# The RWKV scan of a hybrid encoder: inverse blocks reordered, DMAs merged, one engine's stores moved, the hand-written order of the pieces changed

## The chip, the cores and the metric

The kernel runs on one core of a Trainium2 chip. The metric is the device time of one execution in microseconds (us), the median of the runs shown; lower is better. The core has TensorE (PE, with PEld for its weight loads), VectorE (DVE), ScalarE (ACT), GpSimd (POOL) and SyncE (SP), each with its own instruction queue that runs in program order. All DMAs of the kernel before but one are issued from SP's queue.

## What is computed

Two layers, each a token mixer and a convolutional feed-forward block on a residual of 512 tokens by 1024 channels in float32. Layer 0 mixes by windowed attention, layer 1 by the bidirectional RWKV-7 scan, 16 heads of 64, and the change is in that scan alone. Its core:

```python
def wkv7_scan(r, w, k, v, a, bb, reverse):
    ...
    def step(state, inp):
        r_t, w_t, k_t, v_t, a_t, b_t = inp
        sa = jnp.einsum('bhvk,bhk->bhv', state, a_t)
        state = state * w_t[:, :, None, :] + sa[..., None] * b_t[:, :, None, :] + v_t[..., None] * k_t[:, :, None, :]
        y = jnp.einsum('bhvk,bhk->bhv', state, r_t)
        return state, y
    s0 = jnp.zeros((b, nh, n, n), F32)
    _, y = lax.scan(step, s0, seq, reverse=reverse)
    return jnp.moveaxis(y, 0, 1)
...
    y_f, bonus_f = direction(0)
    y_b, bonus_b = direction(1)
    y = y_f + y_b
```

After the scan come a norm per head, a bonus term, a gate and the output projection `w_o`.

## The kernel before, in words

Activations are held transposed, [channel, token]; channels come in KT = 8 tiles of 128, so one "tile of heads" is two heads (e = 0, 1) in two directions (d = 0, 1). Tokens are cut into NC = 8 chunks of 64. The time recurrence is rewritten by chunk: inside a chunk it is a triangular system, so for each chunk, head and direction a 64x64 unit triangular matrix has to be inverted. It is split into two halves h of 32: 2 halves x 2 directions x 8 chunks x 2 heads = 64 blocks of 32x32 for one tile of heads.

`rwkv_proj` (L432) makes the operands and stores them to DRAM (`ars`, `bks`, `vs`); near its end it already runs the first pieces of the scan for two tiles of heads (`stages`, L1172). `rwkv_scan.run` (L1209) then runs the scan, software-pipelined: i goes from -1 to 7, and in each i the eight strings of `K.between` (L1313) are played out, one per chunk step j. I call the strings slots 0 to 7, and the time from one w0 to the next a period. The pieces of a string:

- c: `step` (L1106), chunk step j of tile i: state matmuls (L1115, L1119), the products of the next chunk (`added`, L1104), and on VectorE the decay of the state (L1117), on which the matmuls of the next step wait.
- l0 to l3: `low` (L928), the triangular matrices of tile i+2: matmuls L937, masked eviction on VectorE L939. b: `blocks` (L942) stores the 32x32 blocks to DRAM (`ls`, L946, 4 DMAs) and loads them, one block to a partition, into both halves of the tile X (L950, 2 DMAs, which wait for the stores).
- G3, V5, V6, G4, g4, g5: so many steps of `solve` (L986) on GpSimd (G, g) or VectorE (V). G and V work for tile i+2, g and v for tile i+1. 31 steps (kx = 31 down to 1), each a multiply (L1000) and an add (L1002) over 16 to 136 elements; the 32nd call ends the inverse: four copies X<-Y on ScalarE (L905 by `copy`) and four stores `zs` from SP (L1012).
- I: `inverses` (L1022) loads the inverse blocks back, 2 DMAs for T32 (tile t, L1028) and 8 for TT (tt, L1032); L0, L1: `level` (L1034), the off-diagonal quarter, ends in four copies tt (L905).
- u: the loads vv of the values (L958, 3 DMAs); t0, t1: transposes L966 with copies bw on ScalarE; a0, a1: `sides` (L970, matmuls L976, L978, copies xa, xv on ScalarE); x0, x1 (L1070, copies x, then vv, on ScalarE) and m0, m1 (L1079, VectorE L1082, L1083): `batch` (L1060) for chunks 0-3 and 4-7; w0, w1: `locals_` (L1096).
- n0 to n4: the head norm of tile i-1: square on ScalarE (L1139), sum on VectorE (L1142), power on GpSimd (L1144), scaling on VectorE (L1146), PE transposes (L1151), VectorE L1154, L1155, store os (L1159). e: loads gt, bo. p: `prep` (L913) loads the operands of tile i+3.

At the end of `run` every instruction is chained to the one before it on its engine, so each queue, SP's too, keeps the order in which the pieces stand. `bank()` hands out four PSUM banks in turn; a piece waits until the evictions of the one four banks earlier are done.

Of the kernel before, what the change touches and what calls it, by code (L numbers as in the profile page):

```python
# [8 lines left out]
F32 = mybir.dt.float32  # L9
# [806 lines left out]
def rwkv_scan(K, A, sc, mid):  # L816
# [9 lines left out]
    MID = ("gc", "ks", "mask", "id2", "t", "gt", "bo")  # L826
    PLACE = {"early": ("bw0", "ar0", "ar1", "bk0", "bk1", "X0", "Y0", "tg", "tv"),
             "ring": ("bw1", "ar2", "ar3", "bk2", "bk3", "xa0", "vv", "mt0", "qt0", "mt1", "qt1", "st", "rv", "tt0", "Q", "x10", "x11", "t32"),
             }
# [4 lines left out]
    def qr(e, h):  # L834
        return slice(HD * e + 32 * h, HD * e + 32 * h + 32)
# [34 lines left out]

    GROUPS = [(hf, d) for hf in range(2) for d in range(2)]
    BOTH = [(d, e) for d in range(2) for e in range(2)]
# [16 lines left out]
    def inputs(n, bks=True):  # L889

        for _ in range(n):
            for _ in range(2):
                R.ARs.append(mk([P, 2, NC, HD], f"ar{len(R.ARs)}"))
                if bks:
                    R.BKs.append(mk([P, NC, 2, HD], f"bk{len(R.BKs)}"))
            R.BWs.append(mk([P, 2, NC, 2, 3 * HD], f"bw{len(R.BWs)}").rearrange("p d c e s -> p c d e s"))
# [16 lines left out]
    def prep(ct):  # L913

        c = Ctx()
        c.AR, c.BK = [], []
        for d in range(2):
            c.AR.append(R.ARs[(2 * ct + d) % len(R.ARs)])
            nc.sync.dma_start(out=c.AR[d], in_=sc["ar"][ct, d])
            c.BK.append(R.BKs[(2 * ct + d) % len(R.BKs)])  # L920
            nc.sync.dma_start(out=c.BK[d], in_=sc["bk"][ct, d])
        return c
# [18 lines left out]

    def blocks(ct, c):  # L942

        for d in range(2):
            for h in range(2):
                nc.sync.dma_start(out=sc["l"][ct, d, h].rearrange("c e i j -> i c e j"),  # L946
                                  in_=c.BW[qr(d, h), :, d, :, 32 * h:32 * h + 32])
        c.X = block()
        for h in range(2):
            nc.sync.dma_start(out=c.X[er(h)], in_=sc["l"][ct].rearrange("d h c e i j -> (d h c e) i j"))  # L950

# [34 lines left out]
    def solve(ct, c):  # L986
# [18 lines left out]
        for h in range(2):  # L1005
            yh = Y[HD * h:HD * h + HD]
            copy("z0", h, Z[0:HD].rearrange("p i (j h) -> p i j h", h=2)[:, :, :, h], yh)
            copy("z1", h, Z[HD:P].rearrange("p (j h) i -> p j h i", h=2)[:, :, h], yh.rearrange("p i j -> p j i"))
        zd = sc["z"][ct]
        for i, d in ((0, 0), (0, 1), (1, 0), (1, 1)):  # L1010
            p0 = d + HD * (i == 0)
            nc.sync.dma_start(out=zd[i, :, d], in_=Z[p0:p0 + HD - d:2])  # L1012

# [158 lines left out]
    def stages(names):  # L1172

        for x in names:
            ct = R.done[x]
            R.done[x] += 1
            K.ct = ct
            if x == "p":
                R.cs.append(prep(ct))
            elif x == "l":  # L1180
                for g in range(4):
                    low(ct, R.cs[ct], g)
                blocks(ct, R.cs[ct])
            else:
                go(ct, R.cs[ct], 32, "G")
# [5 lines left out]
    def part(i, q):  # L1191
# [69 lines left out]
def body(ctx, tc, A, out, stage=9):  # L1261
# [109 lines left out]
    def ffn(layer, xT, st, nxt, nst, store):  # L1371
# [152 lines left out]
```

## Time and profile before

| | us |
|---|---|
| median of 3 runs | 1620.83 |
| lowest, highest | 1620.26, 1624.76 |
| the profiled execution | 1621.33 |
| its span | 1619.5 |
| the scan's periods (first to last w0 in the trace) | 926.9 to 1165.3 |
| PE busy over the span | 92% |
| DVE, ACT, POOL busy over the span | 63%, 43%, 28% |
| granted TensorE clock, mean | 0.938 |

The span is the part of the execution with instructions in it; 1.8 us lie around it. Outside the scan PE is busy nearly all the time; the slices in which it is not, and in which the granted clock falls to about half and then hovers around eight tenths, are those from about 850 to 1200 us.

### The profile page before, as it was taken

The numbers are of one execution on the slowest core, as the hardware profiler recorded it, in microseconds if no ns is written. First come the engines' busy times: TensorE is split into PE (matmuls) and PEld (weight loads), VectorE is DVE, ScalarE is ACT, GpSimd is POOL, SyncE is SP. The second block draws the span as 40 slices with busy tenths as digits, with TensorE's granted clock in tenths as the row PEclk, the third lists the DMA queues.
The fourth block names the chain that finished last, engine by engine and source line by source line (L and its number), as shares of the span: only waits on it lengthen the run. The fifth ranks groups of instructions, "written<-read, shape, count | busy, mean of one in ns | idle before, by whom it ended". The sixth has DMA issues, their size and how long they took to land.

```text
span 1619.5 us, 28606 instructions
## 1 busy us (share of the span) xinstructions
PE 1494.3 (92%) x11612; PEld 1203.0 (74%) x11612; DVE 1024.9 (63%) x1652; ACT 689.1 (43%) x1147; POOL 449.7 (28%) x546
## 2 busy tenths in 40 slices
PE   8999999999999998989987588888689999999999
PEld 7767688888888886667765477777567788888887
DVE  6876447777763348968878556676256677777222
ACT  5576434444442223655545243434324444444111
POOL 2630002322210015425696423334100323222000
PEclk9999999999999999999975688888789999999999
DMA  5200032232333322346627545555532222333331
GB/s 192 73 27 1 25 94 92 91 103 93 100 91 119 112 81 71 127 156 234 206 88 225 156 117 150 151 136 145 160 106 82 88 92 94 93 103 101 100 121 56
DMA packets 110131, 180.15 MB, mean 111 GB/s; under 512 B 50096, under 2 KB 63024, under 8 KB 110000
## 3 DMA queue, kind: packets, MB, share of 16 engines
q1 hardware_dynamic: 109856, 178.33, 36.0%
q8 instruction: 91, 1.49, 0.4%
q14 instruction: 40, 0.33, 0.1%
q10 hardware_dynamic: 144, 0.00, 0.0%
HBM read 142.91 MB, written 35.39 MB: 110 GB/s over the span
## 4 chain that ended last, share of the span: by engine, by line
PE 69%; DVE 11%; DMA 6%; POOL 5%; issue 4%; ACT 4%; SPq 1%; POOLq 0%; ACTq 0%; DVEq 0%
PE mm L106 16%; PE mm L104 16%; PE mm L105 16%; PE mm L387 2%; PE sc L104 2%; PE sc L105 2%; PE sc L106 2%; PE tp L382 2%; DVE wlo L71 2%; POOL Y L1002 1%; POOL tg L1000 1%; PE sc L367 1%; DMA X<-ls 1%; DVE sf L530 1%; PE bank L1096 1%
## 5 line engine op out<-in xcount | busy, mean ns | idle before, releaser
L68 ACT CAST whi<-wraw 128x1024 fp32r<-128x1024 f32 (+2 forms) x196 | 200.4, 1023 | 270.2 <-PE mm L105 178.4
L104 PE MATMUL mm<-hl,whi 128*128 128x512 f32 x720 | 281.7, 391 | 1.5 <-DVE xT L1354 0.9
L106 PE MATMUL mm<-hl,wlo 128*128 128x512 f32 x720 | 281.5, 391 | 0.6 <-POOL wlo L71 0.4
L105 PE MATMUL mm<-hl,whi 128*128 128x512 f32 x720 | 281.4, 391 | 0.4 <-DVE hl L92 0.4
L71 DVE TENSOR_TENSOR wlo<-wraw,whi 128x1024 fp32r<-128x1024 f32 (+2 forms) x139 | 170.7, 1228 | 174.6 <-ACT whi L68 173.9
L71 POOL TENSOR_TENSOR wlo<-wraw,whi 128x1024 fp32r<-128x1024 f32 x57 | 137.1, 2406 | 414.8 <-ACT whi L68 414.8
L185 DVE SCALAR_TENSOR_TENSOR conv<-upad,par,conv 128x512 f32<-128x512 f32 x88 | 125.6, 1429 | 64.0 <-ACT conv L182 64.0
L106 PEld LDWEIGHTS mm<-hl,wlo 128*128 128x128 f32 x720 | 135.6, 188 | 31.9 <-POOL wlo L71 2.3
L104 PEld LDWEIGHTS mm<-hl,whi 128*128 128x128 f32 x720 | 135.7, 189 | 29.6 <-ACT hl L91 1.3
L105 PEld LDWEIGHTS mm<-hl,whi 128*128 128x128 f32 x720 | 135.7, 189 | 29.5 <-DVE hl L92 1.1
L106 PE MATMUL mm<-gh,wlo 128*128 128x512 f32 x352 | 139.0, 395 | 0.0
L104 PE MATMUL mm<-gh,whi 128*128 128x512 f32 x352 | 139.0, 395 | 0.0
L105 PE MATMUL mm<-gl,whi 128*128 128x512 f32 x352 | 139.0, 395 | 0.0
L1000 POOL TENSOR_TENSOR tg<-X,Y 128x56 f32<-128x56 f32 (+9 forms) x136 | 51.5, 379 | 142.4 <-DMA X<-ls 67.9
L97 ACT CAST gh<-gact 128x512 fp32r<-128x512 f32 x44 | 27.3, 621 | 141.4 <-DVE gact L194 141.4
L182 ACT ACTIVATE conv<-upad,par 128x512 f32<-128x512 f32 x88 | 71.6, 815 | 21.5 <-DVE upad L180 21.3
L106 PEld LDWEIGHTS mm<-gh,wlo 128*128 128x128 f32 x352 | 66.1, 188 | 16.1
L105 PEld LDWEIGHTS mm<-gl,whi 128*128 128x128 f32 x352 | 66.1, 188 | 16.0
L104 PEld LDWEIGHTS mm<-gh,whi 128*128 128x128 f32 x352 | 66.1, 188 | 16.0
L187 DVE SCALAR_TENSOR_TENSOR conv<-upad,par,conv 128x512 f32<-128x512 f32 x88 | 70.0, 798 | 3.0
L192 ACT ACTIVATE silu<-conv 128x512 f32<-128x512 f32 x44 | 27.8, 632 | 91.3 <-DVE conv L187 91.3
L106 PE MATMUL mm<-sx,wlo 128*128 128x512 f32 (+1 forms) x144 | 59.9, 416 | 5.2 <-DVE wlo L71 5.0
(334 smaller groups left out, 3078.5 us busy)
## 6 DMA issues: line engine op xcount, KB each, us to landing
wraw<-in_w_up_dram SPq DMA_DIRECT2D x88, 512.0 KB, 3.6
wraw<-in_w_down_dram SPq DMA_DIRECT2D x32, 512.0 KB, 3.5
ars<-tab SPq DMA_DIRECT2D x16, 512.0 KB, 2.7
bks<-tab SPq DMA_DIRECT2D x16, 512.0 KB, 3.0
ar<-ars SPq DMA_DIRECT2D x16, 512.0 KB, 5.1
bk<-bks SPq DMA_DIRECT2D x16, 512.0 KB, 6.4
wraw<-in_w_down_dram SPq DMA_DIRECT2D x16, 384.0 KB, 3.2
wraw<-in_w_qkv_dram SPq DMA_DIRECT2D x11, 512.0 KB, 4.5
```

The lines of the kernel that those rows point to most:

```text
L68: nc.scalar.copy(out=hi, in_=raw)
L71: lo_engine.tensor_tensor(out=lo, in0=raw, in1=hi.bitcast(F32), op=ALU.subtract)
L104: nc.tensor.matmul(ps, lhsT=lhs[0], rhs=rhs[0], start=first, stop=False)
L105: nc.tensor.matmul(ps, lhsT=lhs[0], rhs=rhs[1], start=False, stop=False)
L106: nc.tensor.matmul(ps, lhsT=lhs[1], rhs=rhs[0], start=False, stop=last)
L182: nc.scalar.activation(out=c, in_=u[:, 1:S + 1], func=AF.Identity, scale=K.par[:, cw + 2 * FT + ch:cw + 2 * FT + ch + 1], bias=K.par[:, cb ...
L185: nc.vector.scalar_tensor_tensor(out=c, in0=u[:, 0:S], scalar=K.par[:, cw + ch:cw + ch + 1], in1=c, op0=ALU.mult, op1=ALU.add)
L187: nc.vector.scalar_tensor_tensor(out=c, in0=u[:, 2:S + 2], scalar=K.par[:, cw + 4 * FT + ch:cw + 4 * FT + ch + 1], in1=c, op0=ALU.mult, op ...
L192: nc.scalar.activation(out=sg, in_=acts[0], func=AF.Silu)
L382: nc.tensor.transpose(out=tp[:, j * P:(j + 1) * P], in_=p[:, e, j * P:(j + 1) * P], identity=K.ident)
L387: nc.tensor.matmul(po[e * HD:(e + 1) * HD, n], lhsT=vn[:, n - 1 + j, kv * HD:(kv + 1) * HD], rhs=pT[:, e, j * P:(j + 1) * P], start=n == 0 ...
L1000: en.tensor_tensor(out=tm, in0=X[:, 0:kx, kx:kx + 1].broadcast_to([P, kx, n]), in1=Y[:, kx:kx + 1, m:16].broadcast_to([P, kx, n]), op=ALU. ...
```

## The change

Three things are changed in the data and one in the order. The 64 blocks are ordered (half, direction, chunk, head) where they were (direction, half, chunk, head); the stores `ls` of one direction are issued as soon as its two `low` pieces are done (b0, b1, with GROUPS reordered to go by direction); the inverse goes back to DRAM in 3 DMAs issued by ScalarE, holding of the transposed part only the blocks that are read (384 KB where it was 512 KB); TT is loaded in 4 DMAs of twice the size. The operands AR and BK of both directions come in one DMA each. TT has two buffers, its copies alternate between ScalarE and VectorE. Both x pieces and a1 stand late in the period before, and the steps of the inverse are dealt out anew.

```diff
-    GROUPS = [(hf, d) for hf in range(2) for d in range(2)]
+    GROUPS = [(hf, d) for d in range(2) for hf in range(2)]
...
-            for _ in range(2):
-                R.ARs.append(mk([P, 2, NC, HD], f"ar{len(R.ARs)}"))
-                if bks:
-                    R.BKs.append(mk([P, NC, 2, HD], f"bk{len(R.BKs)}"))
+            R.ARs.append(mk([P, 2, 2, NC, HD], f"ar{len(R.ARs)}"))
+            if bks:
+                R.BKs.append(mk([P, 2, NC, 2, HD], f"bk{len(R.BKs)}"))
...
-        for d in range(2):
-            c.AR.append(R.ARs[(2 * ct + d) % len(R.ARs)])
-            nc.sync.dma_start(out=c.AR[d], in_=sc["ar"][ct, d])
-            c.BK.append(R.BKs[(2 * ct + d) % len(R.BKs)])
-            nc.sync.dma_start(out=c.BK[d], in_=sc["bk"][ct, d])
+        nc.sync.dma_start(out=bk, in_=sc["bk"][ct].rearrange("d p c z s -> p d c z s"))
+        nc.sync.dma_start(out=ar, in_=sc["ar"][ct].rearrange("d p z c s -> p d z c s"))
...
-    def blocks(ct, c):
-
-        for d in range(2):
-            for h in range(2):
-                nc.sync.dma_start(out=sc["l"][ct, d, h].rearrange("c e i j -> i c e j"),
-                                  in_=c.BW[qr(d, h), :, d, :, 32 * h:32 * h + 32])
-        c.X = block()
+    def blocks(ct, c, d):
+
         for h in range(2):
-            nc.sync.dma_start(out=c.X[er(h)], in_=sc["l"][ct].rearrange("d h c e i j -> (d h c e) i j"))
+            nc.sync.dma_start(out=sc["l"][ct, h, d].rearrange("c e i j -> i c e j"),
+                              in_=c.BW[qr(d, h), :, d, :, 32 * h:32 * h + 32])
+        if d:
+            c.X = block()
+            for b in range(2):
+                nc.sync.dma_start(out=c.X[er(b)], in_=sc["l"][ct].rearrange("h d c e i j -> (h d c e) i j"))
...
+            copy("z1", h, Z[HD:P].rearrange("p (j h) i -> p j h i", h=2)[:, :, h], yh.rearrange("p i j -> p j i"))
+        for h in range(2):
+            yh = Y[HD * h:HD * h + HD]
             copy("z0", h, Z[0:HD].rearrange("p i (j h) -> p i j h", h=2)[:, :, :, h], yh)
-            copy("z1", h, Z[HD:P].rearrange("p (j h) i -> p j h i", h=2)[:, :, h], yh.rearrange("p i j -> p j i"))
         zd = sc["z"][ct]
-        for i, d in ((0, 0), (0, 1), (1, 0), (1, 1)):
-            p0 = d + HD * (i == 0)
-            nc.sync.dma_start(out=zd[i, :, d], in_=Z[p0:p0 + HD - d:2])
+        for d in range(2):
+            nc.scalar.dma_start(out=zd[0, 48 * d:48 * d + 16], in_=Z[HD + 48 * d:HD + 48 * d + 16])
+        nc.scalar.dma_start(out=zd[1], in_=Z[0:HD])
...
-        for e in range(2):
-            for h in range(2):
-                for d in range(2):
-                    nc.sync.dma_start(out=c.TT[qr(e, h), :, d, 32 * h:32 * h + 32], in_=zs[1, d, h, :, e].rearrange("c i j -> i c j"))
+        for h in range(2):
+            for e in range(2):
+                nc.sync.dma_start(out=tt[qr(e, h), :, :, 32 * h:32 * h + 32].rearrange("p d c s -> p (d c) s"),
+                                  in_=sc["z"][ct, 1, 32 * h + e:32 * h + 32:2].rearrange("b i j -> i b j"))
...
-        R.TTs = [mk([P, NC, 2, HD], "tt0")]
-        eng("zero").memset(R.TTs[0], 0.0)
+        R.TTs = [mk([P, 2, NC, HD], f"tt{i}") for i in range(2)]
+        for t in R.TTs:
+            eng("zero").memset(t, 0.0)
...
         if x in "xm":
-            k, fn, args = i + (args[0] == 0), batch, [args[0], int(x == "m")]
+            k, fn, args = i + (q != "m1"), batch, [args[0], int(x == "m")]
...
-    K.between = ("w0 c l0 l1 u g4", "c l2 l3 b e g5", "c x1 I", "c m1 w1 n0 G3", "c t0 t1 n1 V5", "c a0 a1 n2 V5 p", "c L0 n3 V6", "c L1 x0 n4 m0 G4")
+    K.eng["tt"] = "CV"
+    K.between = ("w0 c l0 l1 b0 u g5", "c l2 l3 g6 b1 I", "c m1 w1 n0 e", "c t0 t1 n1 G4", "c a0 p V5 n2", "c L0 n3 V4", "c L1 a1 n4 G4", "c x0 x1 m0 G4")
```

## Rows read from the trace of the kernel before

**Rows 1.** Windows of the periods: us, busy by engine (x count), PEclk, DMA share, GB/s.

```profile
1133.10:1165.30 32.20, 25.15 (x675) 21.48 (x672) 9.13 (x23) 14.04 (x30) 6.41 (x17) 0.82 0.43 109
sum 238.40, PE 200.28 PEld 173.26 DVE 139.45 ACT 98.65 POOL 76.39; mean PE 28.61 PEld 24.75 DVE 19.92 ACT 14.09 POOL 10.91
```

**Rows 2.** PE's waits, 910 to 1175 us: total us, times, longest.

```profile
PE bank L1104 <- ACT vv L905: 12.8, 14, 4.7
PE bank L1119 <- DVE st L1117: 5.3, 4, 2.1
PE pre L1044 <- DMA tt<-zs: 2.6, 2, 1.5
```

**Rows 3.** Timeline, one period from 1031.7: start, us; the blocks to DRAM and back.

```profile
1038.92 2.04 SPq L946 DMA_DIRECT2D ls<-bw  x4
1042.72 1.11 SPq L950 DMA_DIRECT2D X<-ls  x2
1048.37 0.25 POOL L1000 TENSOR_TENSOR tg<-X,Y 128x31 f32<-128x31 f32 x1 [12.52 <-DMA X<-ls]
```

**Rows 4.** Timeline, the same period: the inverse, VectorE, GpSimd and ScalarE.

```profile
1050.35 1.65 POOL L1144 TENSOR_TENSOR rv<-rv,mhalf 128x8 f32<-128x8 f32 x1
1053.29 0.68 DVE L1146 TENSOR_TENSOR t<-t,rv 128x512 f32<-128x512 f32 x1
1061.20 0.41 POOL L1000 TENSOR_TENSOR tg<-X,Y 128x120 f32<-128x120 f32 x1 [9.20 <-DVE Y L1002]
1061.75 0.90 DVE L1155 TENSOR_TENSOR t<-t,gt 128x512 f32<-128x512 f32 x1
1062.19 0.74 POOL L1000 TENSOR_TENSOR tg<-X,Y 128x121 f32<-128x121 f32 x1
1071.44 3.47 ACT L905 COPY X<-Y 64x512 f32<-64x512 f32 x4 [7.52 <-POOL Y L1002]
```

**Rows 5.** Timeline, 1039 to 1063: PE's pieces, and ScalarE's copies behind them.

```profile
1039.37 1.10 PE L1070 MATMUL mm<-xa,tt 64*64 64x128 f32 x32
1050.87 1.07 ACT L905 COPY xa<-mm 128x512 f32<-128x512 f32 x2 [1.01 <-PE mm L976]
1052.58 1.07 ACT L905 COPY xa<-pre 128x512 f32<-128x512 f32 x2 [0.63 <-PE pre L978]
1054.52 1.15 PE L1151 MATMUL bank<-ident,t 64*64 64x64 f32 x32
1057.67 0.75 PE L1044 MATMUL mm<-tt,Q 32*32 32x32 f32 x64
1058.94 3.13 PE L1070 MATMUL pre<-xa,tt 64*64 64x128 f32 x32 [0.51 <-ACT tt L905]
1062.38 1.54 ACT L905 COPY vv<-pre 64x256 f32<-64x256 f32 x4
```

**Rows 6.** Groups by form, 900 to 1140: a solve operation on VectorE and GpSimd, mean ns.

```profile
L1000 DVE TENSOR_TENSOR tv<-X,Y 128x126 f32<-128x126 f32 x21 | 6.0, 288 | 0.5
L1002 POOL TENSOR_TENSOR Y<-Y,tg 128x121 f32<-128x121 f32 x7 | 2.9, 418 | 0.6
```

**Rows 7.** Windows, columns as in Rows 1: the vv loads in the DMA queues.

```profile
1032.00:1034.00 2.00, 2.00 (x54) 1.93 (x52) 1.61 (x5) 0.00 (x0) 1.56 (x6) 0.84 1.00 205
1034.00:1036.00 2.00, 2.00 (x48) 1.84 (x44) 1.09 (x2) 0.91 (x2) 1.52 (x7) 1.00 0.10 16
```

**Rows 8.** DMA issues: KB each, median us to landing.

```profile
vv<-vs SPq DMA_DIRECT2D x8, 256.0 KB, 7.0
```

**Rows 9.** Windows, columns as in Rows 1: PE's longest wait and the clock behind it.

```profile
1138.80:1142.00 3.20, 0.00 (x0) 0.00 (x0) 0.25 (x1) 2.89 (x4) 0.22 (x1) 0.98 0.00 0
1143.50:1148.60 5.10, 4.81 (x72) 4.07 (x72) 1.56 (x5) 1.03 (x3) 0.00 (x0) 0.50 0.68 137
```

**Rows 10.** Timeline ahead of the scan, 877 to 901 us: SP's queue and VectorE.

```profile
877.09 3.81 SPq L1012 DMA_DIRECT2D zs<-X  x4
900.79 1.72 DVE L766 TENSOR_TENSOR tab<-tr,ts 128x512 f32<-128x512 f32 x1 [5.57 <-DMA ars<-tab]
```

More of the change, by code (lines that the diff above doesn't have):

```diff
@@ L826, in rwkv_scan @@
     MID = ("gc", "ks", "mask", "id2", "t", "gt", "bo")
-    PLACE = {"early": ("bw0", "ar0", "ar1", "bk0", "bk1", "X0", "Y0", "tg", "tv"),
-             "ring": ("bw1", "ar2", "ar3", "bk2", "bk3", "xa0", "vv", "mt0", "qt0", "mt1", "qt1", "st", "rv", "tt0", "Q", "x10", "x11", "t32"),
+    PLACE = {"early": ("bw0", "ar0", "bk0", "X0", "Y0", "tg", "tv"),
+             "ring": ("bw1", "ar1", "bk1", "xa0", "vv", "mt0", "qt0", "mt1", "qt1", "st", "rv", "tt0", "tt1", "Q", "x10", "x11", "t32"),
              }
@@ L915, in prep @@
         c = Ctx()
-        c.AR, c.BK = [], []
-        for d in range(2):
-            c.AR.append(R.ARs[(2 * ct + d) % len(R.ARs)])
-            nc.sync.dma_start(out=c.AR[d], in_=sc["ar"][ct, d])
-            c.BK.append(R.BKs[(2 * ct + d) % len(R.BKs)])
-            nc.sync.dma_start(out=c.BK[d], in_=sc["bk"][ct, d])
+        ar, bk = R.ARs[ct % len(R.ARs)], R.BKs[ct % len(R.BKs)]
+        c.AR, c.BK = [ar[:, d] for d in range(2)], [bk[:, d] for d in range(2)]
+        nc.sync.dma_start(out=bk, in_=sc["bk"][ct].rearrange("d p c z s -> p d c z s"))
+        nc.sync.dma_start(out=ar, in_=sc["ar"][ct].rearrange("d p z c s -> p d z c s"))
         return c
@@ L1022, in inverses @@
     def inverses(ct, c):
-        zd = sc["z"][ct]
         c.T32 = mk([P, NC, 2, 32], "t32", 1)
-        c.TT = R.TTs[ct % K.ntt]
-        zs = zd.rearrange("x (d h c) e i j -> x d h c e i j", d=2, h=2)
+        tt = R.TTs[ct % len(R.TTs)]
+        c.TT = tt.rearrange("p d c s -> p c d s")
         for d in range(2):
-            nc.sync.dma_start(out=c.T32[qr(d, d)], in_=zs[0, d, d].rearrange("c e i j -> i c e j"))
-        for e in range(2):
-            for h in range(2):
-                for d in range(2):
-                    nc.sync.dma_start(out=c.TT[qr(e, h), :, d, 32 * h:32 * h + 32], in_=zs[1, d, h, :, e].rearrange("c i j -> i c j"))
+            nc.sync.dma_start(out=c.T32[qr(d, d)].rearrange("p c e s -> p (c e) s"), in_=sc["z"][ct, 0, 48 * d:48 * d + 16].rearrange("b i j -> i b j"))
+        for h in range(2):
+            for e in range(2):
+                nc.sync.dma_start(out=tt[qr(e, h), :, :, 32 * h:32 * h + 32].rearrange("p d c s -> p (d c) s"),
+                                  in_=sc["z"][ct, 1, 32 * h + e:32 * h + 32:2].rearrange("b i j -> i b j"))
     def level(ct, c, k):
@@ L1182, in stages @@
                     low(ct, R.cs[ct], g)
-                blocks(ct, R.cs[ct])
+                for d in range(2):
+                    blocks(ct, R.cs[ct], d)
             else:
@@ L1378, in body @@
           "bo": dram.tile([KT, P, S], F32, name="bos"), "o": dram.tile([KT, P, S], F32, name="os"),
-          "l": dram.tile([KT, 2, 2, NC, 2, 32, 32], F32, name="ls"), "z": dram.tile([KT, 2, 32, 2, 32, 32], F32, name="zs")}
+          "l": dram.tile([KT, 2, 2, NC, 2, 32, 32], F32, name="ls"), "z": dram.tile([KT, 2, HD, 32, 32], F32, name="zs")}
     st = {}
```

## The prediction

> **What bounds the kernel now.** I read the page's slices first: PE is busy nearly throughout except from about 850 to 1200 us, the scan, which is all that the change touches. Then the windows from one w0 to the next. Seven periods take 238.40 us, 34.1 each, PE is busy 28.6 of them, and the last, in which no new inverse is begun, takes 32.2; the six with one average 34.4 [rows 1]. A busy PE is not yet a bound here: x0 takes 3.13 us where the same 32 matmuls as x1 take 1.10 [rows 5], the granted clock being 1.2 GHz in the one and 2.4 in the other, beside a first matmul that waits for copies. At full clock and without waits PE would need some 24 us of a period (28.6 by the granted 0.84 or so).
>
> So a period is set by chains that go once round through the in-order queues. PE's waits name their ends: for ScalarE's vv copies, for the state on VectorE, for the TT loads [rows 2]. The timeline of one period shows the links. From w0 at 1031.7 the blocks' stores start at 7.2 us, the X loads are issued at 11.0 and GpSimd begins to solve at 16.7, having idled for it [rows 3]. Three steps later (2.0) VectorE takes over, does sixteen steps, and GpSimd resumes at 29.5 and ends at 39.7, when ScalarE begins the four copies, 3.5 us [rows 4]. Those copies stand ahead of x1's copies on ScalarE, which is why PE waits for vv, 12.8 us in all [rows 2].
>
> **The change, part by part.**
>
> Merged and moved DMAs. SP issues per tile fall from 30 to 20 (TT 8 to 4, operands 4 to 2, the inverse's 4 to ScalarE); the bytes of the inverse fall by a quarter. In the steady scan this takes TT's landing off PE's path (2.6 us in all, [rows 2]), some 0.4 a period. Ahead of the scan it is worth more: the four z stores hold SP for 3.81 us, and VectorE later sits 5.57 us behind an operand store that queued after such traffic [rows 10]. I take 4.5 us off there; bounds 0 (another wait ends last) and 6. On ScalarE three issues cost, by SP's own, 0.51 each (ls, [rows 3]) to 0.95 (z, [rows 10]); I take 1.5 us, since the queue it goes to is empty.
>
> A rule that speaks against this part: the Trainium skill, DMA: Bandwidth & Descriptors, section Issuing engines are not separate DMA queues, says that DMAs started on different engines end on the same 16 DMA engines, and that a second issuer saves only the sequencer's time. By that rule the move is worth the issue time alone; the sum above takes no more.
>
> x1 out of the wait. x1 goes from slot 2 to slot 7 of the period before, ahead of the inverse's copies. PE's 12.8 us of waiting for vv over seven tiles, 1.8 a period, go. What is late next is the subject of the rest.
>
> The step counts. Per tile VectorE does 9 steps where it did 16, GpSimd 22 where it did 15. An operation of this size takes 288 ns on VectorE and 418 on GpSimd [rows 6]; a step is (61.2 - 50.4 - 1.3 for three other operations) / 16 = 0.59 us on the one and, for the largest that GpSimd does now, 62.19 - 61.20 = 0.99 on the other [rows 4]. Seven steps at 0.4 us: 2.8 us more in the chain of the inverse.
>
> Another rule against it: the Trainium skill, SBUF — State Buffer, section Who interferes with whom, says that a VectorE instruction with two SBUF inputs and a GpSimd instruction that reads SBUF exclude each other. The trace agrees: the one GpSimd operation that meets L1155 takes 0.74 us where its neighbour takes 0.41 [rows 4]. More solve steps on GpSimd meet L1155 and L1146; that would add 0.3 a period, which I leave in the range.
>
> The new order, slots 0 to 5. Here I expect the loss. PE now does, ahead of n3: w0, six chunk steps, l0 to l3, m1, w1, t0, t1, a0, L0. That is x1 and a1 less than before, and the vv wait less: against n3 at 22.8 us after w0 now (1054.52, [rows 5]), less 1.1 (x1), 1.7 (a1), 1.8 (vv) and 0.8 (the wait for the state, 5.3 over seven, [rows 2]), PE stands before n3 at 17.4. But n3 needs n2, and n2 stands on VectorE behind V5, V5 behind G4 on GpSimd, G4 behind X. The X loads need the last stores of b1, which need the last eviction of l3: nothing of that chain is shortened. So n3 can begin at X + 2.7 (four steps at 2.0/3) + 2.9 (five at 0.59) + 0.7 (L1146): X + 6.3, or 23.0 us with X at 16.7. **PE idles 5.6 us in one piece.**
>
> X itself may come later. In SP's order u now stands behind b0, whose stores wait for the evictions of l0 and l1 (some 5.5 us after w0, by estimate: the first stores of now, which need l2 too, start at 7.2, [rows 3]), where it stood behind nothing. Its loads are 512 KB in short packets and land 7.0 us after issue [rows 8]; now they fill the DMA engines for about 2 us (share 1.00) and are over by 1034 [rows 7], well before the stores of the blocks at 1038.9. Issued at about 6.6 to 8.5 us they run just ahead of b1's stores and X on the same queue. Bounds: 0, if they are through, and 3; I take 1.5, so X at 18.2.
>
> Slots 5 to 7. Behind n3 stand n3 1.15, a chunk step and L1 0.8 each, a1 1.7 (the second pair of xa copies starts 1.7 after the first), the xa copies 1.07, x0 1.10, then, since x0, x1 and m0 take turns on four banks, six copies x and vv at 1.54/4 each, 2.3, which hide x1, and m0 1.1 like x1 [rows 5]: 10.0 us. The period at full clock is 18.2 + 6.3 + 10.0 = 34.5; with X at 16.7, 33.0.
>
> The clock. After PE's longest wait the granted clock is at 0.50 for 5.1 us of work behind it, having been at 0.98 while PE stood still [rows 9]. A wait of 5.6 to 7 us in every period does the same, and the work in those 5.1 us takes half of that longer: 2.5 us. What shorter waits cost at the period's end they cost today too (x0 at 3.13). **Period: 34.5 + 2.5 = 37.0**, against 34.4.
>
> The sum. Six periods by 2.6 is 15.6. Off: 4.5 ahead of the scan; at the end of the scan the last tile's inverse comes back by fewer DMAs, 2 (0 to 4). On: x1 in the first round, 1.5. 15.6 - 4.5 - 2 + 1.5 = +10.6. The profiled execution took 1621.33 us, 0.5 above the median; its span with 1.8 around it would become 1632, the median 1631.
>
> **The rivals.** First, faster. If u's loads don't delay X and the clock recovers early (PE's stretch behind n3 not slowed), the period is set by another chain round GpSimd and ScalarE: eighteen GpSimd steps, twelve of which take 10.2 and the six larger ones 1.0 each, 16.2; the copies 3.5 [rows 4]; three issues 1.5; the square and sum of the norm, by L1146's size 0.7 each, 1.4; the power 1.65; G4 2.7; V5 2.9; L1146 0.7; V4 2.4 [rows 4]: 33.0, with state operations and hops 33.7. That is a floor whatever PE does. Six times -0.7, and -5 around it: -9, 1612. It decides from a PE stretch behind n3 of at most 10.5 us. For it: every edit in isolation removes a wait. Against it: the wait of 5.6 us and what the clock does behind one.
>
> Second, no change: the clock costs 2.5 but X stays at 16.7: 35.5, six by 1.1 = 6.6, less 5: 1622. For it: the vv loads are only 2 us of full queue, and today's run behind 2 MB of operand loads.
>
> Third, worse: the clock stays low to the end of the period, as it is at x0 and m0 now: the 6 us of PE work behind n3 cost up to 4.5 rather than 2.5: 39.0, six by 4.6 = 27.6, less 5: 1643.
>
> That the change does nothing (merged loads off the path, queues still in the same chain) falls under the second: it would give 1620 to 1622.
>
> **How the numbers follow.** Forecast, 1631: 0.38. Faster, 1612: 0.30. No change, 1622: 0.22. Worse, 1643: 0.10. Faster by over 0.3% (4.9 us, about what can be told from no change) has the first rival, 0.30; within 0.3% the second, 0.22; slower 0.48. The range goes from 1606, the faster case with 6 us won ahead of the scan and 4 at its end, to 1641, the forecast with half of the worse case: 1606 to 1641. For slower alone 1626 to 1643.
>
> **What would show it.** Right: PE idle 4 us or more before L1151 in every period, released by L1146; the 0.50 clock behind it; the vv loads in the queue between the two pairs of ls stores; GpSimd's first solve step 17.5 or more after w0. No PE wait for vv is left. Wrong: periods of 34 or less, or L1151 reached by PE only after 22 us, so that nothing waits there. The part ahead of the scan is right if the first w0 comes before 926.9 by 2 us or more.

## The result

The changed kernel takes 1642.36 us (median of four runs, 1641.39 to 1642.77) where the kernel before takes 1620.55 (four runs on the same chip). The ratio is 1.0129, 95% interval 1.011 to 1.0148. The forecast was 1631, 1606 to 1641: the direction is right, the loss is twice what was forecast.

Where it went is read from the windows between one w0 and the next. First the kernel before, in three stretches (first period, the five that carry a whole tile, the last); then the changed kernel. Columns are those of [rows 1]: start:end, us, busy by engine, PEclk, DMA share, GB/s.

```profile
926.90:959.00 32.10, 27.03 (x707) 23.39 (x704) 18.02 (x55) 13.61 (x29) 8.28 (x28) 0.87 0.49 129
959.00:1133.10 174.10, 148.10 (x3683) 128.39 (x3680) 112.31 (x315) 71.00 (x150) 61.69 (x171) 0.84 0.53 138
```

```profile
928.40:963.90 35.50, 24.87 (x706) 22.22 (x704) 15.08 (x43) 12.78 (x28) 13.02 (x40) 0.86 0.48 121
963.90:1156.00 192.10, 134.11 (x3682) 119.16 (x3681) 97.32 (x255) 67.20 (x141) 91.39 (x241) 0.83 0.53 124
1156.00:1185.00 29.00, 21.87 (x676) 19.05 (x674) 9.99 (x25) 13.36 (x29) 8.03 (x21) 0.88 0.34 82
```

The first w0 comes 1.5 us later, the first period is 3.4 longer, the five full periods 18.0 (38.4 each where they took 34.8), the last 3.2 shorter than that of [rows 1], and what follows 1.2 longer: 20.9, the difference of the two spans (1640.4 and 1619.5). In the five, PE is busy 14 us less at about the same granted clock and GpSimd 30 more: the time is waiting.

The waits of PE from 928 to 1156 (total, times, longest), in answer to [rows 2]:

```profile
PE bank L1149 <- DVE t L1144: 22.4, 5, 4.6
PE pre L1039 <- DMA t<-zs: 12.4, 4, 4.8
PE mm L1039 <- DMA t<-zs: 12.3, 5, 4.8
PE bank L1113 <- DVE st L1115: 5.3, 6, 4.1
```

The row for vv that led [rows 2] is gone, as is that for TT; what is left of waiting for vv are twelve waits of at most 0.5 before m0 and m1 (L1077), 5.0 us in all. In their place PE stands still twice in each full period: 4.4 to 4.6 us before n3 (L1149), which was forecast, and 2.4 to 4.8 before L0 (L1039), for T32, which was not. The two have one cause, and it is on SyncE's queue. One period, w0 at 1040.3, answering [rows 3] (start, us; SyncE, then ScalarE, then GpSimd):

```profile
1045.60 0.86 SPq L942 DMA_DIRECT2D ls<-bw  x2
1046.56 1.94 SPq L955 DMA_DIRECT2D vv<-vs  x3
1053.08 0.90 SPq L942 DMA_DIRECT2D ls<-bw  x2
1055.96 1.57 SPq L947 DMA_DIRECT2D X<-ls  x2
1057.58 1.11 SPq L1026 DMA_DIRECT2D t<-zs  x2
...
1048.48 2.87 ACT L904 COPY X<-Y 64x512 f32<-64x512 f32 x3 [7.18 <-POOL Y L999]
1050.67 1.26 ACTq L1010 DMA_DIRECT2D zs<-X  x2
1052.03 0.45 ACTq L1011 DMA_DIRECT2D zs<-X  x1
...
1061.29 0.25 POOL L997 TENSOR_TENSOR tg<-X,Y 128x31 f32<-128x31 f32 x1 [4.65 <-DMA X<-ls]
```

The last block of l3 is evicted 8.0 us after w0, and the queue is free at 1048.5. Yet b1's two stores are issued only 12.8 us after w0, X 15.7 (11.0 before, [rows 3]), and the first solve step comes at 21.0 instead of 16.7. The waits of SyncE's queue say for what:

```profile
SPq L942 <- DMA zs<-X: 23.6, 8, 4.5
SPq L947 <- DMA ls<-bw: 8.1, 8, 1.8
```

The ls stores wait 23.6 us for DMAs of zs, which they neither read nor write. The built program tells why. Each DMA, whichever engine issues it, adds to one of eight counters in turn, and waits until the DMA eight numbers before it, the last on its counter, has landed. The numbers are given when the program is built, by the order in which the builder reckons that the DMAs will be issued. It reckons the three z stores ahead of the period's first ls store; on the chip ScalarE issues them 5 us behind it. One period of the listing (number, issuer, counter, what it waits for):

```
332 ACT zs<-X  counter 3   the copies of Z, 324 tt<-zs
333 ACT zs<-X  counter 4   325 tt<-zs
334 ACT zs<-X  counter 5   the copies of Z, 326 tt<-zs
335 SP  ls<-bw counter 6   l0, l1 and 327 gt<-gs
336 SP  ls<-bw counter 7   328 bo<-bos
...
340 SP  ls<-bw counter 3   l2, l3 and 332 zs<-X
341 SP  ls<-bw counter 4   333 zs<-X
342 SP  X<-ls  counter 5   335, 336, 340, 341 and 334 zs<-X
```

So the blocks of tile i+2 wait for the inverse of tile i+1 to be stored. With the z stores on SyncE, as before, the numbers could not run ahead of the queue.

### The profile page after: what moved, and what is told of

Its sections match the earlier page's. It is cut to its first block, busy times and chain, and to the rows that moved or that the text cites. A ratio compares the mean times of both kernels' runs of the same rounds, so it can differ in the third digit from the quotient of the medians.

```text
span 1640.4 us, 28397 instructions
## 1 busy us (share of the span) xinstructions
PE 1476.3 (90%) x11612; PEld 1191.6 (73%) x11612; DVE 1006.3 (61%) x1570; ACT 683.5 (42%) x1131; POOL 491.8 (30%) x645
## 3 DMA queue, kind: packets, MB, share of 16 engines
q8 instruction: 91, 1.49, 0.4%
## 5 line engine op out<-in xcount | busy, mean ns | idle before, releaser
L997 POOL TENSOR_TENSOR tg<-X,Y 128x56 f32<-128x56 f32 (+20 forms) x185 | 70.4, 381 | 93.4 <-DVE Y L999 42.8
L999 POOL TENSOR_TENSOR Y<-Y,tg 128x56 f32<-128x56 f32 (+20 forms) x185 | 77.6, 420 | 13.3
```

The source lines that it names most:

```text
L997: en.tensor_tensor(out=tm, in0=X[:, 0:kx, kx:kx + 1].broadcast_to([P, kx, n]), in1=Y[:, kx:kx + 1, m:16].broadcast_to([P, kx, n]), op=ALU. ...
L999: en.tensor_tensor(out=Y[:, 0:kx, m:16], in0=Y[:, 0:kx, m:16], in1=tm, op=ALU.add)
```

## The experiments

Two theories for the five periods. **N**, the numbered wait: solve, Z, z store, ls store, X and the next solve have become a closed loop (a chain that comes back to its own first step one tile later), and its length is the period. **O**, the order, the prediction's reason: X is late for the vv loads ahead of it, and PE waits for n2 behind V5. For the stretch ahead of the scan the theories come below. In this table the times are read from each trace; "X" is the first solve step after w0 and "n3" its start after w0, both the mean of the five full periods. The ratio is that of all runs; the times are those of one execution, which can lie some us off its kernel's median (e7's 3.4 below, e3's 3.0 below, e8's 3.6 above); if all of that lay in the scan, it would be up to 0.6 us a period. The first w0 of the changed kernel and of e3 are 1.0 apart, though the engines do the same up to there.

| kernel | ratio to before, 95% | first w0 | first period | a full period | X | n3 |
|---|---|---|---|---|---|---|
| before | 1 | 926.9 | 32.1 | 34.8 | 16.7 | |
| changed | 1.0129 (1.0110 to 1.0148) | 928.4 | 35.5 | 38.4 | 20.9 | 27.2 |
| e1 | 1.0089 (1.0074 to 1.0104) | 930.5 | 35.8 | 36.5 | 18.3 | 24.6 |
| e2 | 1.0095 (1.0077 to 1.0113) | 928.4 | 35.3 | 36.6 | 16.9 | 23.6 |
| e3 | 1.0143 (1.0126 to 1.0160) | 927.4 | 35.5 | 37.6 | 21.4 | |
| e7 | 1.0052 (1.0035 to 1.0069) | 928.9 | 36.3 | 34.4 | 16.7 | 23.0 |
| e4 | 1.0044 (1.0028 to 1.0059) | 927.3 | 34.9 | 35.8 | | |
| e5 | 1.0024 (1.0012 to 1.0036) | 925.7 | 35.4 | 34.8 | | |
| e8 | 0.9984 (0.9971 to 0.9998) | 926.8 | 33.3 | 34.1 | | |
| e9 | 0.9964 (0.9951 to 0.9976) | 926.4 | 32.9 | 32.9 | | |
| e10 | 0.9960 (0.9948 to 0.9972) | 927.2 | 30.9 | 32.8 | | |
| e14 | 0.9938 (0.9918 to 0.9959) | 923.9 | 32.8 | 33.1 | | |

### e3: n2 ahead of V5

```
-"c a0 p V5 n2"
+"c a0 p n2 V5"
```

> One word of slot 4 moved: n2 ahead of V5; the rest is the changed kernel. N: the wait makes a loop without slack, solve, Z, z store, ls store, X, solve of the next tile (38.3 us from first step to first step); only n2's 0.7 leaves it, TensorE's wait before n3 goes but comes back elsewhere: total 1642 - 4 = 1638 (1634 to 1642). O: n3's wait of 4.4 us a period is what the change costs, and it goes: total 1616 (1610 to 1622).

Measured: 1.0143, no faster than the changed kernel (1.0129; the intervals overlap). PE's wait for n2 is gone from the list, and its time turned up in other rows:

```profile
PE bank L1113 <- DVE st L1115: 16.1, 11, 4.1
PE mm L1039 <- DMA t<-zs: 11.8, 3, 4.9
PE pre L1039 <- DMA t<-zs: 9.4, 4, 4.4
```

The loop is seen on GpSimd, at the first solve step of two tiles running:

```profile
1022.52 0.25 POOL L997 TENSOR_TENSOR tg<-X,Y 128x31 f32<-128x31 f32 x1 [3.87 <-DMA X<-ls]
...
1059.80 0.25 POOL L997 TENSOR_TENSOR tg<-X,Y 128x31 f32<-128x31 f32 x1 [4.27 <-DMA X<-ls]
```

37.3 us, against 38.3 in the changed kernel (1023.0 to 1061.29): shorter by the 0.7 of n2 that stood in it, and a little more. N said just that of the loop; the 4 us that it expected off the total show in the traced execution (1637.94), not in the median (1640.92). O, which expected 26 us off the total, is refuted. The wait that was forecast is real, and taking it away is worth nothing that these runs show while the loop holds.

### e1, e2 and e7: the numbered wait taken away, in three ways

e1 issues the z stores from SyncE again, behind X:

```
-"c l2 l3 g6 b1 I"
+"c l2 l3 b1 g6 I"
-            nc.scalar.dma_start(out=zd[0, ...
+            nc.sync.dma_start(out=zd[0, ...
-        nc.scalar.dma_start(out=zd[1], in_=Z[0:HD])
+        nc.sync.dma_start(out=zd[1], in_=Z[0:HD])
```

> The three z stores go back to SyncE and b1 stands ahead of g6, so that on SyncE's queue the ls stores and the X loads come before them; the rest is the changed kernel. In the listing of the changed kernel every DMA adds to one of eight counters in turn and waits until the eighth before it has landed; the z stores are numbered ahead of the period's first ls store, so b1's stores and the X loads wait for the z stores of the tile before. Numbered wait (N): here that wait is gone, the X loads are issued 11 to 12 us after w0 instead of 15.7, the first solve step comes 17 +- 1 after w0 instead of 21.0, n3 at 23.3, the period is 33.9 instead of 37.9; total 1642 - 24 = 1618 (1612 to 1626). Order (O), the prediction's reason: X is late because of the vv loads ahead of it and the period because V5 stands ahead of n2; ScalarE's issues are cheap, so moving them back changes little: first step still after 20, total 1639 to 1646.

e2 leaves them on ScalarE, makes them two, and puts the vv loads behind X, so that all of ls and X are within eight numbers of the z stores:

```
-"w0 c l0 l1 b0 u g5", "c l2 l3 g6 b1 I"
+"w0 c l0 l1 b0 g5", "c l2 l3 g6 b1 u I"
-        for d in range(2):
-            nc.scalar.dma_start(out=zd[0, 48 * d:48 * d + 16], in_=Z[HD + 48 * d:HD + 48 * d + 16])
+        nc.scalar.dma_start(out=zd[0], in_=Z[HD:P])
```

> The z stores stay on ScalarE, in two DMAs (the 64 rows of half 0 at once, 32 of them unused), and u (the vv loads) comes behind b1, so that the eighth before each ls store and X load is a DMA of the period before. N: first solve step 16.7 +- 1 after w0, T32 a little earlier than with the stores on SyncE, period 33.6, total 1616 (1610 to 1624). O: the vv loads' 1.5 us ahead of X go, nothing else: first step 19.5, total 1633 (1629 to 1637).

e7 has the two z stores of e2, but u as the first word of slot 0, so that the vv loads are issued and numbered ahead of everything:

```
-"w0 c l0 l1 b0 u g5"
+"u w0 c l0 l1 b0 g5"
```

> The changed kernel, with u as the first word of slot 0 and the z stores in two DMAs, so that the eighth DMA before each ls store and X load is one that landed long ago, and vv is not late as it was in e2. N with the prediction's own sum: first solve step 16.7 after w0, n3 6.3 later at 23.0 behind V5, then 11.3 to the next w0: period 34.3 (to 35.5 if the clock falls further), total 1.0129 - 6 x 3.2 / 1620 = 1.001 of the kernel before (0.997 to 1.006). O: as e1 and e2, 1.009.

Measured: X comes at 18.3, 16.9 and 16.7 us after w0 where N expected 16 to 18, 16.7 and 16.7, and the period falls to 36.5, 36.6 and 34.4. e7's period is the one that N forecast (34.3), and in this trace it is below that of the kernel before. Its ratio, 1.0052, is near the upper end of what was expected (0.997 to 1.006): the stretch ahead of the scan and the first period are longer than in the kernel before, 6 us together, and the last period is 3.6 shorter. The traced execution (1623.63, the lowest of six; median 1627.04) is only 2.3 us above that of the kernel before; what the slower ones lose besides, this trace can't tell. e1 and e2 gave about half of what N expected of the period and a quarter of what it expected of the total; e2's total (1633.59) is even the one that O named, but its first solve step is not (16.9, O 19.5). Their waits say why. In e1 T32 stands behind the z stores on SyncE, and in e2 the vv loads land after PE wants them. e1's first two rows, then e2's:

```profile
PE mm L1039 <- DMA t<-zs: 18.2, 6, 6.2
PE pre L1039 <- DMA t<-zs: 13.4, 6, 4.2
```

```profile
PE pre L975 <- DMA vv<-vs: 17.9, 3, 6.9
PE mm L975 <- DMA vv<-vs: 15.7, 3, 5.5
```

What e1 and e7 look like on SyncE's queue (w0 at 1001.7 and at 1032.1):

```profile
1006.97 0.86 SPq L942 DMA_DIRECT2D ls<-bw  x2
1007.92 1.95 SPq L955 DMA_DIRECT2D vv<-vs  x3
1009.97 1.09 SPq L942 DMA_DIRECT2D ls<-bw  x2
1014.55 1.12 SPq L947 DMA_DIRECT2D X<-ls  x2
```

```profile
1037.43 3.55 SPq L942 DMA_DIRECT2D ls<-bw  x4
1044.02 1.70 SPq L947 DMA_DIRECT2D X<-ls  x2
```

In both the second pair of stores goes out with the eviction, 8.3 and 8.0 us after w0. From e1 to e7 the vv loads leave the place between the two pairs, and X comes 1.6 earlier: that is the prediction's term for u (1.5), as far as two runs tell that differ in the z stores' issuer as well. From the changed kernel to e1 it comes 2.6 earlier: that is the numbered wait. In e7, PE still waits before n3, 19.2 us in five times, as the prediction had it.

### e4 and e5: the data alone, in the old order

e4 has the merged loads, ScalarE's stores and the new block order, with the strings and step counts of the kernel before:

```
-K.between = ("w0 c l0 l1 b0 u g5", "c l2 l3 g6 b1 I", ...
+K.between = ("w0 c l0 l1 u g4", "c l2 l3 b0 b1 e g5", "c x1 I", "c m1 w1 n0 G3", "c t0 t1 n1 V5", "c a0 a1 n2 V5 p", "c L0 n3 V6", "c L1 x0 n4 m0 G4")
-            k, fn, args = i + (q != "m1"), batch, [args[0], int(x == "m")]
+            k, fn, args = i + (args[0] == 0), batch, [args[0], int(x == "m")]
```

> The changed kernel's data, merged loads and ScalarE's z stores with the slot order and the piece counts of the kernel before (b0 and b1 together in slot 1). Z is ready 6.9 us after w0 there, so its stores have landed before X asks for its counter. Both theories put the loss into the order: total 1616 (1608 to 1622), periods 34.0. A third, that the merged transfers or ScalarE's issues themselves cost, expects 1630 or more.

Measured 1.0044: neither. One cause showed in PE's waits, 5.5 us in three for tt copies that the change had put on VectorE, where the old order has six solve steps ahead of them. e5 puts them back:

```
-    K.eng["tt"] = "CV"
+    K.eng["tt"] = "C"
```

> The old slot order with the changed data (as e4), and the copies of tt back on ScalarE. In e4 TensorE's x0 waited for tt copies on VectorE that stood behind the six steps V6 (5.5 us in three waits). Theory DVE (the split of the tt copies is what e4 lost): six periods go from 213.8 to about 206, total 0.998 of the kernel before, 1615 where that takes 1618 (1611 to 1619). Rival: the merged transfers themselves or ScalarE's z issues cost: total stays above 1.003, 1623 or more.

Measured 1.0024, between the two expectations (0.998, and above 1.003): the tt copies were about half of e4's loss, and the rest stays. The windows of e5 place it:

```profile
925.70:961.10 35.40, 25.70 (x709) 22.63 (x706) 18.11 (x55) 13.53 (x29) 10.38 (x34) 0.84 0.54 121
961.10:1135.00 173.90, 146.04 (x3685) 126.28 (x3682) 112.41 (x315) 71.25 (x150) 58.97 (x165) 0.85 0.52 131
```

The five full periods take 173.9 us, 174.1 before: the merged loads give nothing there, and cost nothing. So of the changed kernel's loss the order and the numbered wait have the 18.0 of the five periods. The first period takes 3.3 us more in e5 and 3.4 more in the changed kernel, but not for one reason. In e5 PE stops for 3.3 us ahead of x0 where the profile finds no releaser (2.7 in e4; more on such stops in the last section); in the changed kernel there is no such stop, and PE waits there for T32 (5.0) and for the state on VectorE (4.1). The data's share in the 3.4 is not shown.

### e6, e12 and e13: the stretch ahead of the scan

The prediction took 4.5 us off it. What ends there is the multiply L421 on GpSimd, on which PE waits and which itself waits for a load of values (tf). It starts at the same time in both kernels, first that of before (its row names another DMA; the tf load lands at 899.48 there and at 899.80 in the changed kernel):

```profile
899.70 1.04 POOL L421 TENSOR_TENSOR tf<-tf,tbs 128x512 f32<-128x512 f32 x1 [7.16 <-DMA ars<-tab]
```

```profile
899.92 1.04 POOL L421 TENSOR_TENSOR tf<-tf,tbs 128x512 f32<-128x512 f32 x1 [1.76 <-DMA tf<-vs]
```

And SyncE's queue ahead of that load in the changed kernel, in answer to [rows 10]:

```profile
887.64 1.18 SPq L1026 DMA_DIRECT2D t<-zs  x2
891.03 0.98 SPq L942 DMA_DIRECT2D ls<-bw  x2
893.82 1.11 SPq L947 DMA_DIRECT2D X<-ls  x2
894.98 0.59 SPq L416 DMA_DIRECT2D tf<-vs  x1
```

The 3.81 us that SyncE spent on z stores are gone, and the queue stands still from 880.3 to 887.6 instead: tile 0's inverse ends 9 us later (its Z copies start at 883.6, 874.6 before), since its X is issued at 797.9 instead of 791.6. e6 brings that inverse forward, by loading tile 0's operands by direction again:

```
+        if ct == 0:
+            for d in range(2):
+                nc.sync.dma_start(out=ar[:, d], in_=sc["ar"][ct, d])
+                nc.sync.dma_start(out=bk[:, d], in_=sc["bk"][ct, d])
+            return c
```

> The changed kernel with the operands of tile 0 alone loaded by direction again, in four DMAs into the same buffers. Theory P (the merged load waits for the stores of both directions, so that tile 0's first block product misses its turn on TensorE, X of tile 0 comes 6 us later and its inverse 9 us later, which keeps what the cheaper z stores gave): the first X is issued at 791 to 793 instead of 797.9, first w0 at 923 (921 to 925) instead of 928.4, total 5 us under the changed kernel. Rival S (SyncE's order of loads behind T32 sets the end of that stretch): first w0 at 928 +- 1, total as the changed kernel.

Measured: the Z copies start 5.2 us earlier and L421 2.0 earlier (897.88), but the first w0 comes at 927.4, only 1.0 earlier, where P expected 923; the ratio is unchanged, 1.0133. P falls. e12 instead takes tile 0's Z copies off ScalarE, where they stand ahead of the activations that tile 1's last blocks wait for:

```
-    K.eng["tt"] = "CV"
+    K.eng.update({"tt": "CV", "z0/0": "G", "z1/0": "G"})
```

> The changed kernel; the four Z copies of tile 0 alone on GpSimd instead of ScalarE. In the changed kernel they stand on ScalarE for 3.5 us ahead of an activation on which VectorE waits 4.7 us, and behind that wait stand the last block of tile 1, its ls stores, its X loads and, in SyncE's order, the load that ends the stretch ahead of the scan. Theory C (this chain, and not SyncE's time for the z stores, sets the first w0): first w0 at 925 (924 to 926) instead of 928.4, total 3 us under the changed kernel, ratio 1.011. Rival S (tile 0's own inverse sets it: T32 comes later by the slower copies): first w0 at 928 or later, ratio 1.013 or more.

Measured: tile 1's ls stores go out 4.4 us earlier, L421 starts at 899.91 as ever, and the first w0 comes at 928.6; 1.0151. That theory falls as well. The queue of e12 shows T32 and TT, late by the slower copies, now ahead of the same load:

```profile
886.60 0.83 SPq L942 DMA_DIRECT2D ls<-bw  x2
889.42 2.09 SPq L1026 DMA_DIRECT2D t<-zs  x2
893.02 2.17 SPq L1029 DMA_DIRECT2D tt<-zs  x4
895.24 1.34 SPq L416 DMA_DIRECT2D tf<-vs  x1
```

So tile 0's inverse and tile 1's blocks end on one queue close to each other, and shortening the second shows nothing while the first is there. e13 has both edits:

> The changed kernel with the edits of e6 and e12 together: tile 0's operands loaded by direction, its four Z copies on GpSimd. Theory two chains (tile 0's inverse to T32 and TT, and tile 1's blocks to X, end within 1 us of each other on SyncE's queue, ahead of the load that ends the stretch, so that shortening either alone shows nothing): with both shortened T32 is issued by 885, X by 890, first w0 at 925 (923 to 926.5), total 3 us under the changed kernel. Rival (that load waits for something else than its queue, the buffer it writes or TensorE): first w0 at 927.5 or later in this run too.

Measured: the load is issued at 892.4, L421 starts at 897.3, and the first w0 comes at 926.3, inside what was expected (X, expected by 890, is issued at 891.2); the total, 1.013 (1.0113 to 1.0148), can't tell the 2 us from none. GpSimd in e13:

```profile
895.46 1.85 POOL L762 TENSOR_TENSOR tkd<-tkd,tk 128x512 f32<-128x512 f32 x1 [2.47 <-ACT tkd L673]
897.28 1.49 POOL L421 TENSOR_TENSOR tf<-tf,tbs 128x512 f32<-128x512 f32 x1
```

L421 no longer waits for the load: it follows GpSimd's own L762 at once, as it does in e6. At L421, then, e6 alone brings 2.0 us, e12 none and both 2.6: two chains on SyncE's queue, and behind them the engines' own. No run here got the 4.5 us.

### e8, e9, e10, e11 and e14: is there a version that beats both?

e8 is e7 with n2 ahead of V5 and a1 ahead of L0:

```
-"c a0 p V5 n2", "c L0 n3 V4", "c L1 a1 n4 G4"
+"c a0 p n2 V5", "c a1 L0 n3 V4", "c L1 n4 G4"
```

> As e7, with n2 ahead of V5 in slot 4 and a1 ahead of L0 in slot 5. N: TensorE waits neither for n2 (ready 16 after w0) nor, with a1 in front, much for T32 (landed 19 to 20); what remains is the solve's chain, X 16.7, 2.7 + 2.9 + 2.4 + 16.2, Z and its transfer 9.5, L0 to the next w0 11: two periods in 62 us, so 31 to 32 each; total 1603 where the kernel before takes 1618 (1597 to 1612), ratio 0.991. Rival: taking n2 away from before n3 moves the wait elsewhere as in e3: 1.003 or more.

Measured 0.9984, between the two expectations: with the loop gone, moving n2 and a1 pays, but the period is 34.1 and not 31 to 32. Two of the five full periods (35.5 and 37.9) hold stops of PE that no semaphore explains, 2.5 and 4.9 us; the other three take 31.8 to 32.8. PE's waits are now for states behind V5 (L1112, 10.4 us) and, before a0, for ScalarE's bkt copies, which stand behind the Z copies (L973, 9.0).

e9 moves those copies to VectorE:

```
-    K.eng.update({"w": "VC", "bkt": "C", "bkt/0": "C", ...
+    K.eng.update({"w": "VC", "bkt": "V", "bkt/0": "C", ...
```

e10 in addition puts V5 and V4 behind the chunk steps of slots 5 and 6, and the tt copies on ScalarE:

```
-"c a0 p n2 V5", "c a1 L0 n3 V4", "c L1 n4 G4"
+"c a0 p n2", "c a1 V5 L0 n3", "c V4 L1 n4 G4"
-    K.eng["tt"] = "CV"
+    K.eng["tt"] = "C"
```

e11 makes e9's edit, and no other, in the kernel before.

> As e8, and the copies of bkt (t0 and t1) of all tiles but the first go from ScalarE to VectorE. In e8 TensorE waits 1 to 3 us a period before a0 for these copies, which stand on ScalarE behind the four Z copies (3.5), the z issues and the square. If that wait is on the path, six periods fall from 203.8 by 6 x 2 to about 192: ratio 0.991 to the kernel before (0.987 to 0.995). Rival: VectorE's own queue (n0, n1's sum, n2) takes the place of the wait, or the solve's chain holds the period: 0.996 to 1.001.

> As e9, with V5 and V4 each behind the chunk step of slots 5 and 6 (the state's evictions then stand ahead of the solve steps on VectorE) and all tt copies on ScalarE. In e8 TensorE waited 2.4 to 4.1 us in three of six periods for a state that stood behind V5. If that wait is on the path: 1.5 us a period more than e9, ratio 0.986 (0.981 to 0.992). Rival: GpSimd's G4 starts later by what the steps of VectorE start later (2 to 3 us), Z and T32 with it: as e9 or worse.

> The kernel before with nothing but the copies of bkt moved from ScalarE to VectorE: whether what e9 gains is of the new order or could be had without it. TensorE waits only 0.5 us for these copies there in all, so no change: ratio 0.998 to 1.002. Were ScalarE's load a limit of its own, 0.995 or less.

Measured: e9 0.9964, e10 0.9960, e11 1.0028 (1.0016 to 1.0041). In e9 and e10 the rivals came true, and e11 lies just above what was expected. From e8 to e9 the ratio falls by 0.2%, hardly more than the two intervals allow; in the old order the same move costs 0.3%. e10's edit changes neither the wait nor the time: the wait for the state, which it was to remove, stands at 19.3 us over 15 times in e9 and 18.6 over 10 in e10. e14 is e9 with the two edits of e13 (the loads of tile 0 by direction, its Z copies on GpSimd):

> e9 with the same two edits for tile 0. Two chains: first w0 at 923.5 instead of 926.4, ratio to the kernel before 0.9945 (0.993 to 0.9965). Rival: as e9, 0.9964.

Measured 0.9938 (0.9918 to 0.9959), 1609.06 us beside 1617.97: faster than the kernel before and than the changed one. Its full periods take 33.1 us, and its first w0 comes at 923.9:

```profile
956.70:1122.00 165.30, 135.69 (x3684) 120.36 (x3680) 109.58 (x275) 57.45 (x121) 91.02 (x240) 0.87 0.53 144
```

What holds the period at 33 is another loop, on GpSimd in e9:

```profile
1009.99 0.25 POOL L997 TENSOR_TENSOR tg<-X,Y 128x31 f32<-128x31 f32 x1
...
1040.48 1.65 POOL L1141 TENSOR_TENSOR rv<-rv,mhalf 128x8 f32<-128x8 f32 x1 [5.69 <-DVE rv L1140]
1043.03 0.25 POOL L997 TENSOR_TENSOR tg<-X,Y 128x31 f32<-128x31 f32 x1
```

The first solve step no longer waits for X but stands behind the norm's power on GpSimd, that behind the sum on VectorE, the square and the Z copies on ScalarE, and the steps of the tile before. Four times running it comes round in 33.0 to 33.1 us, in e14 too. That is the chain of the prediction's first rival, summed there to 33.0 (33.7 with state operations and hops): "a floor whatever PE does".

## Why the prediction was wrong, point by point

The terms of the sum beside what the two traces show (us):

| term | forecast | measured |
|---|---|---|
| ahead of the scan, SyncE's queue | -4.5 | +0.2 (L421) |
| x1 in the first round | +1.5 | +1.3 (L421 to the first w0: 28.5, before 27.2; a1 moved as well) |
| the first period | +2.6 | +3.4 |
| five full periods | +13.0 | +18.0 |
| the end of the scan | -2.0 | -2.0 (-3.2 and +1.2) |
| sum | +10.6 | +20.9 |

**The first step that failed is X at 18.2.** The prediction went through SyncE's queue and found the vv loads ahead of X; that term was about right, 1.5 against 1.6 between e1 and e7. It said of ScalarE's issues that they cost 1.5 us "since the queue it goes to is empty", which is right too (1.26 + 0.45). It did not ask what else orders DMAs of two issuers, and so put the wait of the ls stores for the z stores at nothing: 23.6 us in all, and 2.6 a period at X (e1). X came at 20.9, and the full period, forecast as 18.2 + 6.3 + 12.5, was 20.9 + 6.3 + 11.2. With the numbered wait gone (e7), X came at 16.7, n3 at 23.0 and the period was 34.4: the prediction's own sum for X at 16.7, 33.0 with 2.5 for the clock, comes out 1.1 too high.

The rule of the Trainium skill that the prediction weighed here (DMA: Bandwidth & Descriptors, Issuing engines are not separate DMA queues: a second issuer saves only the sequencer's time) points the right way and not far enough. The trace agrees that no more than the issue time was saved, and shows that a second issuer can cost 2.6 us a period when the program's waits are numbered across issuers.

**The second is the 4.5 us ahead of the scan.** The rows were read rightly, but two rows of one stretch, SyncE's 3.81 and VectorE's 5.57 [rows 10], were taken for time on the path without following what the last load of the stretch waits for: with the z stores off the queue it is issued at 894.98, before at 893.94. Its bound of 0 was the answer, nearly.

**n3 behind V5**, the center of the prediction, was right in place and size: n3 starts X + 6.3 in the changed kernel, e1 and e7 alike (27.2 - 20.9, 24.6 - 18.3, 23.0 - 16.7). It was forecast as one wait of 5.6 or more; in the period at 1040.3 PE stands still for 9.2 in two pieces, since T32, behind X on the queue, was late too. As the cause of the loss it falls: e3 takes it away and gains nothing. Only with the loop gone does moving n2, together with a1, pay (e7 1.0052, e8 0.9984).

**The clock** was sized too high, and for slots 5 to 7 the 10.0 as well. The windows of the period at 1040.3, columns as in [rows 1]: the two waits, L0 between them, and what follows.

```profile
1057.00:1061.70 4.70, 0.00 (x0) 0.00 (x0) 0.00 (x0) 0.27 (x1) 0.34 (x2) 0.88 1.10 172
1061.70:1063.20 1.50, 1.39 (x64) 1.15 (x64) 0.00 (x0) 0.00 (x0) 1.19 (x5) 0.50 1.37 190
1063.20:1067.60 4.40, 0.00 (x1) 0.01 (x1) 3.22 (x12) 0.37 (x1) 0.68 (x3) 0.50 0.98 365
1067.60:1078.30 10.70, 9.14 (x282) 8.09 (x282) 5.10 (x15) 4.87 (x14) 6.84 (x15) 0.85 0.28 107
```

The granted clock is at 0.50 (1.2 GHz) behind the first wait, as forecast, and stays there through the second; it is 0.53 in the first 3.4 us behind n3 and 1.00 after. Of the 10.7 us behind n3 it takes 1.6 by estimate (10.7 by 0.15), not 2.5, and at full clock they would be 9.1, not 10.0. The two together hide 1.3 us a period of what X cost.

**The smaller terms.** The merged loads were to give 0.4 a period; e5 shows none. GpSimd's eighteen steps take 16.4 (1032.07 to 1048.44) where the first rival had 16.2. PE's wait for vv before the chunk step is gone, as forecast, but it was misread: of its 12.8 us 5.0 lie in the last period (4.7 in one piece, the wait of [rows 9]) and 7.8 in the six before, 1.3 a period and not 1.8. By these rows that is also what shortens the end of the scan. With the same DMAs and x1 in its old place PE still waits there, 5.1 us in e4 and 7.7 in e5, and the last period takes 32.3 and 33.7; so the -2.0, forecast for fewer DMAs, was met by luck. So was the size of the first period, in which there is no n3 for PE to wait before. Of GpSimd beside L1155 [rows 4] the prediction saw one operation; two meet it, 0.42 us (at 1061.69) and 0.74, and only the second is longer than its neighbours.

Of what was to show it, four signs out of six came: PE idle 4 us or more before L1149, released by L1144; the 0.50 behind it; the vv loads between the two pairs of ls stores; the first solve step after 17.5. A fifth, no wait for vv, came nearly (5.0 us are left). All of them were also what N would show, and none was a sign of the loop. The sixth, the first w0 before 924.9, did not come (928.4). Of the signs of being wrong one came by half: PE reaches L1149 only 22.3 to 23.6 us after w0, having stood before L0, and waits there all the same. The third rival, 1643, comes nearest to the time; its reason, the clock low to the end of the period, is not what happened.

## What to carry to other kernels

When DMAs move to another issuer, read the waits of the built program, not the queues alone: here every DMA waits for the one eight numbers before it, and three stores that ran later than they were numbered closed a loop through work that has nothing to do with them. Before a wait on an engine is priced, look for a loop that doesn't pass through it, from one tile's first step to the next's: where its length is the period, taking the wait away gives nothing (e3). Once that loop is gone, look for the next: the one that e9 and e14 run into could be summed from the rows of the kernel before. A stall that ends a stretch is worth its time only if nothing else ends within that time of it (e6, e12 and e13).

## What the runs showed of the hardware that was not expected

In e8, PE stopped for 4.9 us in the middle of one group of 64 matmuls whose operands were all there:

```profile
1085.22 0.72 PE L1041 MATMUL pre<-tt,Q 32*32 32x32 f32 x61
1090.87 0.31 PE L1041 MATMUL pre<-tt,Q 32*32 32x32 f32 x3 [4.93 <-issue]
```

No semaphore released it. It falls where the two merged operand loads, 2 MB issued at 1081.6, fill the DMA engines, and one of the packets of the instruction queue (91 in the changed kernel's page, 1.49 MB, so 16.4 KB each) ends in it, 1.3 us before PE goes on. The same holds wherever PE stops for more than 1 us between 900 and 1170 us with no semaphore to wait for: 29 times in the sixteen traces, and each time such a packet ends 1.2 to 1.6 us before PE goes on. The Trainium skill (Runtime: NRT & Kernel Launch, Instruction fetch mechanics) says that an engine's instructions are refilled in blocks of 16 KiB by DMA; the size agrees. So PE waited for its instructions in these stops, as far as traces alone can tell. That the refill of e8 was late behind the operand loads is argued, not shown: no run here moved the loads.

The vv loads land 4.2 us after issue in the changed kernel (7.0 before, [rows 8]). They are no longer issued right behind 2 MB of operand loads, which is the likely reason; that gain was lost in the wait that followed.
